# State-space stage of a hybrid encoder step: the samples' state products as four fp32 products on 32 rows each, and the score banks' pair taken as two single banks

## The chip, the cores and the metric

One Trainium2 chip, one of its cores. The metric is the time of one execution on the device in microseconds (us); the kernel before was run three times, and the median counts.

## What is computed

One layer of a streaming encoder runs on 1024 prompt tokens and on 8 samples of 16 tokens. After a modulated norm one projection feeds an attention branch and a state-space branch; the two are merged, projected and added back. The change touches the last line of the state-space scan, as it is done for the samples (one chunk of 16 tokens each, starting from a given state `h0`):

```python
h_new = h * jnp.exp(a_cs[:, -1])[..., None, None] \
    + jnp.einsum('blgn,blgep->bgepn', bk, xdt * to_end[..., None])
```

Per sample and per pair of heads this is a product over 16 tokens: B transposed (128 states by 16 tokens) times the weighted x (16 tokens by 128 values of two heads), added to the decayed state. Everything is float32.

## The kernel before

All tokens of both groups, 1152, lie side by side. The large projections are the bulk of the work: `dense` multiplies one block of 128 output channels at a time, in three groups of 384 tokens (`G3`). Operands are split in two float32r parts (high and low), so that a product is three matmuls for each of the 8 slices of the inner dimension: lines 442, 443 and 445 in the profile. The first two groups of tokens write a bank of the pool `psd` (two banks, tile `d`). The third group, once attention is over (`att_left[0] == 0`), writes one half of the pool `pss` (line 471): one tile `s` of two banks, which attention uses as a pair for its scores. ScalarE, and VectorE behind it, read each group's sums out of the bank: for a convolution's channels lines 1243 and 1244, for the gate z line 1423, for the merge gates line 1355.

Between these matmuls stands the small work. For each of 16 pairs of heads `ssd(p)` has a `main()` that turns x so that tokens lie on partitions (line 1481), builds the prompt's chunk states (L1526), the outputs (L1553, L1560, L1573), and last the samples' new states. These small products use the pool `psg` (four single banks, tile `g`) and are mostly plain fp32.

The samples' 128 tokens (8 of 16) lie on the 128 partitions of `tokb` (B) and `xw` (weighted x). The samples' states are done in four steps `q` of two samples each. Operands are split in high and low parts once more: `hi` and `lo` of B (lines 1496 to 1503, once per group of four pairs, on ScalarE and VectorE), and `xs`, which holds the high part of x on 64 rows and the low part on the other 64 (L1507 on ScalarE, L1508 on VectorE). GpSimd then makes four masked copies of 128x256 (`masked`, L1515) in which all rows but those of one sample are zero, for two samples side by side. A step is two float32r matmuls of all 128 rows by 256 columns (L1598), with B's `hi` and B's `lo`. Steps 0 and 1 fill one bank `g`, steps 2 and 3 another, some microseconds later (`pause(4500)`); after each bank VectorE adds 512 columns to `h0` (L1607), and at the end GpSimd's queue stores `h0` (L1616).

Two things set the order. Python generators write the program: `run` draws from the dense work and lets the small work in by a credit of time, and `pause(...)` holds a piece back. A scheduler then orders each engine's instructions by its own estimate of when they are ready (`schedule_with_timeline_sim=True`). On the chip each engine takes its instructions in that order.

Of the kernel before, what the change touches and what calls it, by code (L numbers as in the profile page):

```python
# [10 lines left out]
ALU = mybir.AluOpType  # L11
# [23 lines left out]
COLS = 53184  # L35
QCOLS = 1024
VCOLS = 6 * 1024
RCOLS = 16 * NT + 4 * 1024 + 1280 + 32
FCOLS = COLS - RCOLS - QCOLS - VCOLS
NQ = 3 * P  # L40

NQL = NQ + 32

C_ID, C_U, C_UB, C_ONE, C_BLK, C_BM, C_SEL, C_S4, C_BM4 = 0, 128, 256, 384, 512, 640, 648, 680, 712
NCONST = 716

PARAMS = [("norm_g", KT), ("b_ada", 24), ("conv_w", NCV * 4), ("conv_b", NCV), ("qk_g", 2), ("dskip", NPAIR),
          ("ssd_g", NPAIR), ("dt_bias", 32), ("a_log", 32)]
# [73 lines left out]
def trunk_kernel(ctx: ExitStack, tc: tile.TileContext, h):  # L122
# [55 lines left out]
    for n, w in PARAMS:  # L178
# [17 lines left out]
    bmask = cst[:, C_BM:C_BM + NB]  # L196
    sel = cst[:, C_SEL:C_SEL + 32]
    sel4 = cst[:, C_S4:C_S4 + 9]
    bmask4 = cst[:, C_BM4:C_BM4 + 4]

    H0 = 0
    W0 = H0 + 16 * NT
# [3 lines left out]
    L_ATT = arena.set_layout(Z0, [("Q", 1, 16 * P), ("T", 5, NT), ("S", 10, 640), ("U", 2, 640), ("K", 4, 512), ("q", 1, 256), ("d", 1, 256),  # L206
                                  ("k", 1, 128), ("p", 1, 128), ("n", 2, 36 + 3 * 16), ("t", 6, 14)])
    L_ATT["Z"] = L_ATT["T"][2:]
    L_SSD = arena.set_layout(Z0, [("X", 1, XW), ("R", 2, 1184), ("t", 8, 36), ("pad", 1, 576), ("T", 9, NT), ("Y", 1, 1184), ("H", 1, 1024),
                                  ("g", 3, G3)])  # L210
    L_HEAD = dict(L_SSD, T=[x for x in L_SSD["T"] if x[0] + x[1] <= Z0 + 7 * NT])
    L_START = arena.set_layout(Z0, [("T", 11, NT), ("ada", 5, 1024), ("e", 2, 256)])
    L_TAIL = arena.set_layout(Z0, [("T", 15, NT)])
# [4 lines left out]
    L_WA = rarena.set_layout(W0, [("w", 2, 1024)])  # L218
    L_QR = rarena.set_layout(W0 + 2 * 1024, [("q", 3, 1024)])
    L_Q = qarena.set_layout(0, [("q", 1, 1024)])  # L220
    L_ST = rarena.set_layout(W0 + 4 * 1024, [("b", 4, P), ("s", 2, P), ("x", 2, 2 * P)])
    L_W3 = varena.set_layout(0, [("w", 2, 3 * 1024)])
    L_W7 = varena.set_layout(0, [("w", 2, 7 * NQL)])
    L_QS = qarena.set_layout(0, [("ada", 1, 1024)])
# [4 lines left out]
    def alloc(lay, tag, cols, cold=None):  # L229
        if lay is L_Q:  # L230
            try:
                return alloc(L_QR, tag, cols)
            except NoSlot:
                pass
        if lay is L_SSD and tag == "H":
            try:
                return Buf(qarena, qarena.alloc(L_QS, "ada", cols), cols)
            except NoSlot:
                pass
        if lay is L_Q or lay is L_QS:  # L240
            return Buf(qarena, qarena.alloc(lay, tag, cols), cols)
        if lay is L_W3 or lay is L_W7 or lay is L_VT or lay is L_VA:
            return Buf(varena, varena.alloc(lay, tag, cols), cols)
        if lay is L_H or lay is L_W or lay is L_WA or lay is L_QR or lay is L_ST:
            return Buf(rarena, rarena.alloc(lay, tag, cols, cold), cols)
        if (lay is L_SSD or lay is L_HEAD or lay is L_TAIL) and tag == "T" or lay is L_HEAD and tag == "Y":
            if v_open[0]:
                try:
                    return alloc(L_VT, "T", cols)
                except NoSlot:  # L250
                    pass
        return Buf(arena, arena.alloc(lay, tag, cols), cols)
# [170 lines left out]
    for x in [h["wall"][i] for i in range(29, 85)] + [h["watt"][i] for i in range(8)] + [h["wssd"][i] for i in range(16)] \  # L423
            + [h["wout"][i] for i in range(8)]:
        job(x)

    def dense(ops, evict, nk=KT, outs=1, last=False, wide=False, order=(0, 1, 2), other=False):

        i = widx[0]
        widx[0] += 1
        hi, lo = yield from w_wait(i)
        if len(jobs[min(i + 1, len(jobs) - 1)]) > 3:
            w_next(i)

        def mm(ps, o, g, k, parts=(0, 1)):
            tok = slice(g * G3, (g + 1) * G3)
            wc = slice((k * outs + o) * P, (k * outs + o + 1) * P)
            kh, kl = ops[k]  # L440
            if 0 in parts:
                nc.tensor.matmul(ps, hi.r[:, wc], kh.r[:, tok], start=k == 0, stop=False)  # L442
                nc.tensor.matmul(ps, hi.r[:, wc], kl.r[:, tok], start=False, stop=False)  # L443
            if 1 in parts:
                nc.tensor.matmul(ps, lo.r[:, wc], kh.r[:, tok], start=False, stop=k == nk - 1)  # L445

        for o in range(outs):
            if wide or (last and o == outs - 1):
                if wide or other:
                    acc = [pg(G3) for _ in range(3)]  # L450
                else:
                    sp = pss.tile([P, 2, 512], F32, tag="s", name=nm("s"))
                    acc = [psd.tile([P, G3], F32, tag="d", name=nm("d")) for _ in range(2)] + [sp[:, 0, :G3]]
                for k in range(nk):
                    while len(ops) <= k:
                        blocked[0] = "operand"
                        yield None
                    for g in range(3):
                        mm(acc[g], o, g, k)
                        if k == nk - 1:  # L460
                            yield from evict(o, g, slice(g * G3, (g + 1) * G3), acc[g]) or ()
                        yield 3 * 162.5
                    if last and o == outs - 1:
                        for x in ops[k]:
                            x.free()
                    if k == 2 and o == 0:
                        w_next(i)
                continue
            for g in order:
                if g == 2 and att_left[0] == 0:  # L470
                    ps = pss.tile([P, 2, 512], F32, tag="s", name=nm("s"))[:, 0, :G3]
                else:
                    ps = psd.tile([P, G3], F32, tag="d", name=nm("d"))
                for k in range(nk):
                    while len(ops) <= k:
                        blocked[0] = "operand"
                        yield None
                    mm(ps, o, g, k)
                    if nk == KT and g == order[-1] and k in (3, 5, 7):
                        w_over(i, k)  # L480
                    yield 3 * 162.5
                yield from evict(o, g, slice(g * G3, (g + 1) * G3), ps) or ()
                if o == 0 and (g == 0 or len(jobs[min(i + 1, len(jobs) - 1)]) > 1):
                    w_next(i)
        w_done(i)
# [876 lines left out]
    grp = {}  # L1362

    def group_dense(g, lay):
        res = grp[g] = {"b": [], "c": [], "sq": None, "st": None}
        yield from conv_gen(16 + g, lay, res["b"])
        yield from conv_gen(20 + g, lay, res["c"])

# [31 lines left out]
    def ssd(p):  # L1400
# [62 lines left out]
        def main():  # L1463
# [24 lines left out]
            me, eb, h0, tm = st["me"]  # L1488
            ssd_all[p + 1] = True

            if res["st"] is None:
                bs = res["st"] = []
                for j in range(2):
                    rw, ro = slice(64 * j, 64 * j + 64), slice(64 - 64 * j, 128 - 64 * j)
                    b_ = tokb.ap[rw, NP:]
                    hi = yield from walloc(L_ST, "b", P)
                    lo = yield from walloc(L_ST, "b", P)
                    nc.scalar.activation(hi.r[rw], b_, AF.Copy)
                    nc.scalar.activation(hi.r[ro], b_, AF.Copy)
                    nc.vector.tensor_tensor(lo.r[rw], b_, hi.ap[rw], ALU.subtract)  # L1500
                    nc.vector.tensor_tensor(lo.r[ro], b_, hi.ap[rw], ALU.subtract)
                    bs.append((hi, lo))
            xs = []
            for j in range(2):
                rw, ro = slice(64 * j, 64 * j + 64), slice(64 - 64 * j, 128 - 64 * j)
                t = yield from walloc(L_ST, "s", P)
                nc.scalar.activation(t.r[rw], xw.ap[rw, NP:], AF.Copy)  # L1507
                nc.vector.tensor_tensor(t.r[ro], xw.ap[rw, NP:], t.ap[rw], ALU.subtract)  # L1508
                xs.append(t)

            def masked(q):

                t = alloc(L_ST, "x", 2 * P)
                i = 2 * (q % 2)
                nc.gpsimd.tensor_tensor(t.r.rearrange("p (b n) -> p b n", n=P), xs[q // 2].ap.unsqueeze(1).to_broadcast([P, 2, P]),  # L1515
                                        bmask4[:, i:i + 2].unsqueeze(2).to_broadcast([P, 2, P]), ALU.mult)
                return t

            xm = [masked(0), masked(1)]

            yield from pause(1500)
            for j in range(2):
# [68 lines left out]
            nc.scalar.activation(z.ap, x.ap, AF.Square)  # L1591
            stored(x)
            yield from pause(2000)
            pss_ = [pg(), pg()]
            for q in range(4):
                j, i = q // 2, q % 2
                for w, b_ in enumerate(res["st"][j]):
                    nc.tensor.matmul(pss_[j][:, 2 * i * P:2 * (i + 1) * P], b_.r, xm[q].r, start=w == 0, stop=w == 1)  # L1598
                xm[q].free()
                if q < 2:  # L1600
                    xm.append(masked(q + 2))
                yield 215
                if q == 1:
                    yield from pause(4500)
                if i:
                    c = slice(4 * j * P, (4 * j + 4) * P)
                    nc.vector.tensor_tensor(h0.ap[:, c], h0.ap[:, c], pss_[j], ALU.add)  # L1607
            for t in xs + [xw]:
                t.free()
            if res["sq"] is None:  # L1610
                res["sq"] = z
            else:
# [4 lines left out]
            stored(h0)  # L1617
            if p % PPG == PPG - 1:
                s = res["sq"]
                for t in (tokb, res["cbm"], res["ct"], *res["st"][0], *res["st"][1]):  # L1620
                    t.free()
                yield from pause(4500)
                r0 = drp.tile([1, NT], F32, name=nm("ya"))
# [301 lines left out]
```

## Time and profile before

| | us |
|---|---|
| three runs | 1956.46, 1957.06, 1957.90 |
| median | 1957.06 |
| span of the profiled execution | 1955.7 |
| TensorE busy in it | 1938.3 |
| state-space stage in it | about 783 to 1530 |

The profile's span runs from the first to the last instruction of one profiled execution. The profile shows no other time of that execution; the median of the runs, which are timed around the whole of it, is 1.4 us longer than this span. PE is TensorE's matmul unit, PEld its weight loads, DVE VectorE, ACT ScalarE, POOL GpSimd. A plain fp32 product is shown as two matmul instructions, a float32r product as one. The duration of a single matmul in the profile is its latency; matmuls overlap, so what one costs is read from the distance between starts.

### The profile page before, as it was taken

Reading aid. Unit: us, or ns where it says so; the run is one execution under the profiler, and the core shown is the slowest. Engines: PE = TensorE matmul, PEld = TensorE weight load, DVE = VectorE, ACT = ScalarE, POOL = GpSimd, SP = SyncE. Lnnn points to the kernel's source line nnn. Section 1 sums busy time; section 2 is a strip of 40 time slices with the busy share of each in tenths; the row PEclk is TensorE's granted clock in tenths of the full one; section 3 lists DMA queues with packets and bytes.
Section 4 is the critical chain, followed back from the end, with each engine's and each line's share of the span. In section 5 each row is a group of like instructions: output and inputs, shape, how many; then the busy total and the mean of one; then the engine's idle time right before and its main releaser. Section 6 shows DMA issues by size and latency. Waiting matters only on the chain.

```text
span 1955.7 us, 35068 instructions
## 1 busy us (share of the span) xinstructions
PE 1938.3 (99%) x14091; PEld 1859.4 (95%) x14091; DVE 1168.5 (60%) x2441; ACT 776.4 (40%) x1589; POOL 323.5 (17%) x624
## 2 busy tenths in 40 slices
PE   7999999999999999999999999999999999999999
PEld 5999999899998999999999999999999999999999
DVE  7455555556555765757566666576674334777732
ACT  8444444445444557344454434345351301111200
POOL 0312213122131201212212221122212100000000
PEclk9999999999999999999999999999999999999999
DMA  9124244232432325433333333332337642331241
GB/s 367 60 81 131 86 132 131 90 122 88 131 112 96 112 88 160 128 112 110 95 132 129 106 103 114 117 118 91 117 118 291 234 140 92 104 104 56 86 143 52
DMA packets 81209, 238.62 MB, mean 122 GB/s; under 512 B 14284, under 2 KB 15320, under 8 KB 81048
## 3 DMA queue, kind: packets, MB, share of 16 engines
q1 hardware_dynamic: 72088, 207.74, 32.7%
q0 software_dynamic: 8960, 28.65, 3.8%
q8 instruction: 111, 1.82, 0.4%
q14 instruction: 50, 0.41, 0.1%
HBM read 192.70 MB, written 43.66 MB: 121 GB/s over the span
## 4 chain that ended last, share of the span: by engine, by line
PE 96%; DVE 1%; ACT 1%; DMA 1%; issue 0%; SPq 0%
PE d L442 13%; PE d L443 13%; PE d L445 13%; PE s L442 5%; PE s L445 5%; PE s L443 5%; PE d L508 5%; PE d L506 5%; PE d L507 5%; PE g L1043 3%; PE g L1066 3%; PE g L1553 2%; PE s L1122 2%; PE g L1526 1%; PE g L1573 1%; PE g L1122 1%
## 5 line engine op out<-in xcount | busy, mean ns | idle before, releaser
L442 PE MATMUL d<-rarena 128*128 128x384 f32 x1520 | 517.4, 340 | 0.3 <-ACT arena L1355 0.3
L445 PE MATMUL d<-rarena 128*128 128x384 f32 x1520 | 511.4, 336 | 0.0
L443 PE MATMUL d<-rarena 128*128 128x384 f32 x1520 | 511.0, 336 | 0.0
L442 PEld LDWEIGHTS d<-rarena 128*128 128x128 f32 x1520 | 285.6, 188 | 4.6 <-issue 2.3
L443 PEld LDWEIGHTS d<-rarena 128*128 128x128 f32 x1520 | 285.6, 188 | 2.8 <-issue 2.4
L445 PEld LDWEIGHTS d<-rarena 128*128 128x128 f32 x1520 | 285.5, 188 | 1.1 <-issue 0.9
L334 ACT ACTIVATE rarena<-arena 128x1024 fp32r<-128x1024 f32 x92 | 97.5, 1060 | 314.1 <-PE s L443 226.2
L442 PE MATMUL s<-rarena 128*128 128x384 f32 x640 | 216.7, 339 | 0.0
L443 PE MATMUL s<-rarena 128*128 128x384 f32 x640 | 214.2, 335 | 0.0
L445 PE MATMUL s<-rarena 128*128 128x384 f32 x640 | 214.1, 334 | 0.0
L508 PE MATMUL d<-va_att,rarena 128*128 128x384 f32 (+1 forms) x559 | 195.0, 349 | 0.0
L506 PE MATMUL d<-va_att,rarena 128*128 128x384 f32 (+1 forms) x559 | 193.9, 347 | 0.0
L507 PE MATMUL d<-va_att,rarena 128*128 128x384 f32 (+1 forms) x559 | 191.0, 342 | 0.0
L335 DVE TENSOR_TENSOR rarena<-arena,rarena 128x1024 fp32r<-128x1024 f32 x92 | 113.2, 1230 | 82.7 <-ACT rarena L334 82.4
L1031 ACT ACTIVATE arena<-arena 128x640 f32<-128x640 f32 (+2 forms) x144 | 101.4, 706 | 138.0 <-DVE arena L1140 99.7
L442 PEld LDWEIGHTS s<-rarena 128*128 128x128 f32 x640 | 120.3, 188 | 1.0 <-issue 1.0
L443 PEld LDWEIGHTS s<-rarena 128*128 128x128 f32 x640 | 120.3, 188 | 0.0
L445 PEld LDWEIGHTS s<-rarena 128*128 128x128 f32 x640 | 120.1, 188 | 0.0
L508 PEld LDWEIGHTS d<-va_att,rarena 128*128 128x128 f32 x559 | 105.5, 189 | 3.9 <-issue 2.7
L1263 DVE SCALAR_TENSOR_TENSOR arena<-arena 128x1176 f32<-128x1176 f32 x66 | 99.9, 1514 | 15.5 <-ACT arena L1260 14.2
L506 PEld LDWEIGHTS d<-va_att,rarena 128*128 128x128 f32 x559 | 105.2, 188 | 3.1 <-issue 1.2
L507 PEld LDWEIGHTS d<-va_att,rarena 128*128 128x128 f32 x559 | 105.2, 188 | 1.0 <-issue 0.4
(345 smaller groups left out, 3212.9 us busy)
## 6 DMA issues: line engine op xcount, KB each, us to landing
arena<-in_wall_dram SPq DMA_DIRECT2D x85, 512.0 KB, 3.9
arena<-in_kc_dram SPq DMA_DIRECT2D x64, 256.0 KB, 4.2
arena<-in_vc_dram SPq DMA_DIRECT2D x64, 256.0 KB, 3.4
arena<-acs_d SPq DMA_DIRECT2D x19, 576.0 KB, 3.8
gate_d<-arena POOLq DMA_DIRECT2D x48, 192.0 KB, 2.5
arena<-y_d SPq DMA_DIRECT2D x15, 576.0 KB, 5.6
arena<-in_wssd_dram SPq DMA_DIRECT2D x16, 512.0 KB, 4.1
arena<-in_wada_dram SPq DMA_DIRECT2D x15, 512.0 KB, 8.9
```

The costliest lines, as they stand in the source:

```text
L334: keep(nc.scalar.activation(hi.r[:, c], b.ap, AF.Copy))
L335: keep(nc.vector.tensor_tensor(lo.r[:, c], b.ap, hi.ap[:, c], ALU.subtract))
L442: nc.tensor.matmul(ps, hi.r[:, wc], kh.r[:, tok], start=k == 0, stop=False)
L443: nc.tensor.matmul(ps, hi.r[:, wc], kl.r[:, tok], start=False, stop=False)
L445: nc.tensor.matmul(ps, lo.r[:, wc], kh.r[:, tok], start=False, stop=k == nk - 1)
L506: nc.tensor.matmul(ps, kh.r[:, tok], wh, start=j == 0, stop=False)
L507: nc.tensor.matmul(ps, kh.r[:, tok], wl, start=False, stop=False)
L508: nc.tensor.matmul(ps, kl.r[:, tok], wh, start=False, stop=j == KT - 1)
L1031: nc.scalar.activation(p, p, AF.Exp, bias=sm_[:, 4 + e:5 + e], scale=-1.0, accum_out=sm_[:, 6 + e:7 + e])
L1043: nc.tensor.transpose(ps[:, s * P:(s + 1) * P], p[:, (j + s) * P:(j + s + 1) * P], ident)
L1122: late(nc.tensor.matmul(banks[k][e][:, o:o + w], x.r[hs, qs], y.r[hs, kk], start=i == 0, stop=i == 2))
L1263: nc.vector.scalar_tensor_tensor(yc, r.ap[:, j:j + n], w4[:, i, j:j + 1], yc, ALU.mult, ALU.add)
```

## The change

The high and low parts of B and x, their layout in the float32r arena, and three of four masked copies go away. GpSimd makes one masked copy `xm` of 128x256 per pair: in each group of 32 rows (two samples) the left 128 columns hold the rows of the first sample and the right 128 those of the second. Four plain fp32 matmuls, one for each group of 32 rows, multiply these 32 rows of B with the same 32 rows of `xm`, each into a bank of its own: three of pool `psg`, and for the fourth one half of the `s` tile. VectorE adds four times 256 columns. The wait of 4500 ns between the halves goes.

`half_pair` allocates the `s` tile once and hands out its two halves in turn, to the fourth product and to the third groups of `dense` in this stage and after it; before, each third group allocated the tile anew and took half 0. The masks and the arenas are sized to fit: 256 columns move from the float32r arena to the plain one. Lines move by 8 to 18: 442, 443, 445 of the kernel before are 452, 453, 455, and the new products are line 1580, their additions 1585.

```diff
+    pair = []
+
+    def half_pair(cols):
+
+        if not pair:
+            sp = pss.tile([P, 2, 512], F32, tag="s", name=nm("s"))
+            pair.extend(sp[:, e, :] for e in range(2))
+        pair.append(pair.pop(0))
+        return pair[-1][:, :cols]
...
                 if g == 2 and att_left[0] == 0:
-                    ps = pss.tile([P, 2, 512], F32, tag="s", name=nm("s"))[:, 0, :G3]
+                    ps = half_pair(G3)
...
-            if res["st"] is None:
-                bs = res["st"] = []
-                for j in range(2):
...
-                    nc.scalar.activation(hi.r[rw], b_, AF.Copy)
-                    nc.scalar.activation(hi.r[ro], b_, AF.Copy)
-                    nc.vector.tensor_tensor(lo.r[rw], b_, hi.ap[rw], ALU.subtract)
-                    nc.vector.tensor_tensor(lo.r[ro], b_, hi.ap[rw], ALU.subtract)
...
-                nc.scalar.activation(t.r[rw], xw.ap[rw, NP:], AF.Copy)
-                nc.vector.tensor_tensor(t.r[ro], xw.ap[rw, NP:], t.ap[rw], ALU.subtract)
-                xs.append(t)
...
-            xm = [masked(0), masked(1)]
+            xm = yield from walloc(lay, "x", 2 * P)
+            nc.gpsimd.tensor_tensor(xm.ap.rearrange("p (b n) -> p b n", n=P), xw.ap[:, NP:].unsqueeze(1).to_broadcast([P, 2, P]),
+                                    parity.unsqueeze(2).to_broadcast([P, 2, P]), ALU.mult)
...
-            pss_ = [pg(), pg()]
-            for q in range(4):
-                j, i = q // 2, q % 2
-                for w, b_ in enumerate(res["st"][j]):
-                    nc.tensor.matmul(pss_[j][:, 2 * i * P:2 * (i + 1) * P], b_.r, xm[q].r, start=w == 0, stop=w == 1)
...
-                if q == 1:
-                    yield from pause(4500)
-                if i:
-                    c = slice(4 * j * P, (4 * j + 4) * P)
-                    nc.vector.tensor_tensor(h0.ap[:, c], h0.ap[:, c], pss_[j], ALU.add)
+            pq = [pg(2 * P) for _ in range(3)] + [half_pair(2 * P)]
+            for r in range(4):
+                rw = slice(32 * r, 32 * r + 32)
+                nc.tensor.matmul(pq[r], tokb.ap[rw, NP:], xm.ap[rw], start=True, stop=True)
+            xm.free()
+            yield 440
+            for r in range(4):
+                c = slice(2 * r * P, 2 * (r + 1) * P)
+                nc.vector.tensor_tensor(h0.ap[:, c], h0.ap[:, c], pq[r], ALU.add)
```

On TensorE, at the second of the 16 pairs, the kernel before has two groups of four products; here is the first (`g` is the bank of steps 0 and 1, `d` the dense work's):

```order
L442 MATMUL d_8704<-rarena 128x384
L443 MATMUL d_8704<-rarena 128x384
L445 MATMUL d_8704<-rarena 128x384
L1598 MATMUL g_8738<-rarena 128x256 x4
L442 MATMUL d_8704<-rarena 128x384
L443 MATMUL d_8704<-rarena 128x384
```

At the same place of the changed kernel stand the four new products, each for 32 rows; `s_7947` is the one `s` tile:

```order
L455 MATMUL d_8678<-rarena 128x384
L1580 MATMUL g_8716<-arena,va_ssd 128x256
L1580 MATMUL g_8717<-arena,va_ssd 128x256
L1580 MATMUL g_8718<-arena,va_ssd 128x256
L452 MATMUL d_8733<-rarena 128x384
L453 MATMUL d_8733<-rarena 128x384
L455 MATMUL d_8733<-rarena 128x384
L1580 MATMUL s_7947<-arena,va_ssd 128x256
L452 MATMUL d_8733<-rarena 128x384
L453 MATMUL d_8733<-rarena 128x384
```

The second group of four is gone, and the fourth new product does not stand with the other three: three dense matmuls were put between. So it is at 11 of the 16 pairs (with 3 to 42 other matmuls between); at the other five, the first, fifth, ninth, fifteenth and sixteenth, the four stand together.

On ScalarE, at the third pair of the kernel before, the reading of the third group's sums (`s`, L1243 and L1244) stands behind a square of 1152 columns, nine pieces of the decay matrix (L1453) and a weight split (L334):

```order
L1457 ACTIVATE arena<-arena 128x1152
L1240 ACTIVATE arena<-d_9046 128x384
L1591 ACTIVATE va_ssd<-arena 128x1152
L1453 ACTIVATE va_ssd<-va_ssd,arena 128x128 x9
L334 ACTIVATE rarena<-arena 128x1024
L1243 ACTIVATE arena<-s_9091 128x256
L1244 ACTIVATE arena<-s_9091 128x8x16
```

In the changed kernel the same reading is L1252 and L1253, the square L1574, the decay matrix L1462:

```order
L1462 ACTIVATE arena<-arena 128x128 x7
L1466 ACTIVATE arena<-arena 128x1152
L1249 ACTIVATE arena<-d_9010 128x384
L1574 ACTIVATE va_ssd<-arena 128x1152
L334 ACTIVATE rarena<-arena 128x1024
L1252 ACTIVATE arena<-s_7947 128x256
L1253 ACTIVATE arena<-s_7947 128x8x16
```

The nine pieces of the decay matrix no longer stand ahead of the reading there; the square and the weight split still do.

More of the change, by code (lines that the diff above doesn't have):

```diff
@@ L37 @@
 VCOLS = 6 * 1024
-RCOLS = 16 * NT + 4 * 1024 + 1280 + 32
+RCOLS = 16 * NT + 5 * 1024 + 32
 FCOLS = COLS - RCOLS - QCOLS - VCOLS
@@ L42 @@
 NQL = NQ + 32
-C_ID, C_U, C_UB, C_ONE, C_BLK, C_BM, C_SEL, C_S4, C_BM4 = 0, 128, 256, 384, 512, 640, 648, 680, 712
-NCONST = 716
+C_ID, C_U, C_UB, C_ONE, C_BLK, C_BM, C_SEL, C_S4, C_PAR = 0, 128, 256, 384, 512, 640, 648, 680, 712
+NCONST = 714
 PARAMS = [("norm_g", KT), ("b_ada", 24), ("conv_w", NCV * 4), ("conv_b", NCV), ("qk_g", 2), ("dskip", NPAIR),
@@ L198, in trunk_kernel @@
     sel4 = cst[:, C_S4:C_S4 + 9]
-    bmask4 = cst[:, C_BM4:C_BM4 + 4]
+    parity = cst[:, C_PAR:C_PAR + 2]
     H0 = 0
@@ L208, in trunk_kernel @@
     L_ATT["Z"] = L_ATT["T"][2:]
-    L_SSD = arena.set_layout(Z0, [("X", 1, XW), ("R", 2, 1184), ("t", 8, 36), ("pad", 1, 576), ("T", 9, NT), ("Y", 1, 1184), ("H", 1, 1024),
-                                  ("g", 3, G3)])
+    L_SSD = arena.set_layout(Z0, [("X", 1, XW), ("R", 2, 1184), ("t", 8, 36), ("x2", 1, 256), ("pad", 1, 320), ("T", 9, NT), ("Y", 1, 1184), ("H", 1, 1024),
+                                  ("g", 3, G3), ("x", 1, 256)])
+    L_SSD["x"] += L_SSD.pop("x2")
     L_HEAD = dict(L_SSD, T=[x for x in L_SSD["T"] if x[0] + x[1] <= Z0 + 7 * NT])
@@ L220, in trunk_kernel @@
     L_Q = qarena.set_layout(0, [("q", 1, 1024)])
-    L_ST = rarena.set_layout(W0 + 4 * 1024, [("b", 4, P), ("s", 2, P), ("x", 2, 2 * P)])
     L_W3 = varena.set_layout(0, [("w", 2, 3 * 1024)])
@@ L243, in alloc @@
             return Buf(varena, varena.alloc(lay, tag, cols), cols)
-        if lay is L_H or lay is L_W or lay is L_WA or lay is L_QR or lay is L_ST:
+        if lay is L_H or lay is L_W or lay is L_WA or lay is L_QR:
             return Buf(rarena, rarena.alloc(lay, tag, cols, cold), cols)
@@ L451, in dense @@
                 else:
-                    sp = pss.tile([P, 2, 512], F32, tag="s", name=nm("s"))
-                    acc = [psd.tile([P, G3], F32, tag="d", name=nm("d")) for _ in range(2)] + [sp[:, 0, :G3]]
+                    acc = [psd.tile([P, G3], F32, tag="d", name=nm("d")) for _ in range(2)] + [half_pair(G3)]
                 for k in range(nk):
@@ L1364, in group_dense @@
     def group_dense(g, lay):
-        res = grp[g] = {"b": [], "c": [], "sq": None, "st": None}
+        res = grp[g] = {"b": [], "c": [], "sq": None}
         yield from conv_gen(16 + g, lay, res["b"])
@@ L1489, in main @@
             ssd_all[p + 1] = True
-            if res["st"] is None:
-                bs = res["st"] = []
-                for j in range(2):
[L1494 to L1497, printed above, removed]
-                    nc.scalar.activation(hi.r[rw], b_, AF.Copy)
-                    nc.scalar.activation(hi.r[ro], b_, AF.Copy)
-                    nc.vector.tensor_tensor(lo.r[rw], b_, hi.ap[rw], ALU.subtract)
-                    nc.vector.tensor_tensor(lo.r[ro], b_, hi.ap[rw], ALU.subtract)
[L1502 to L1508, printed above, removed]
-                xs.append(t)
[L1511 to L1517, printed above, removed]
-            xm = [masked(0), masked(1)]
+            xm = yield from walloc(lay, "x", 2 * P)
+            nc.gpsimd.tensor_tensor(xm.ap.rearrange("p (b n) -> p b n", n=P), xw.ap[:, NP:].unsqueeze(1).to_broadcast([P, 2, P]),
+                                    parity.unsqueeze(2).to_broadcast([P, 2, P]), ALU.mult)
             yield from pause(1500)
@@ L1593, in main @@
             yield from pause(2000)
-            pss_ = [pg(), pg()]
-            for q in range(4):
-                j, i = q // 2, q % 2
-                for w, b_ in enumerate(res["st"][j]):
[L1598 to L1602, printed above, removed]
-                if q == 1:
-                    yield from pause(4500)
-                if i:
-                    c = slice(4 * j * P, (4 * j + 4) * P)
-                    nc.vector.tensor_tensor(h0.ap[:, c], h0.ap[:, c], pss_[j], ALU.add)
-            for t in xs + [xw]:
-                t.free()
+            pq = [pg(2 * P) for _ in range(3)] + [half_pair(2 * P)]
[7 more added lines that the diff above has]
+                nc.vector.tensor_tensor(h0.ap[:, c], h0.ap[:, c], pq[r], ALU.add)
+            xw.free()
             if res["sq"] is None:
@@ L1619, in main @@
                 s = res["sq"]
-                for t in (tokb, res["cbm"], res["ct"], *res["st"][0], *res["st"][1]):
+                for t in (tokb, res["cbm"], res["ct"]):
                     t.free()
@@ L1893 @@
     const[:, C_S4:C_S4 + 32] = (i[:, None] % 32) == np.arange(32)[None, :]
-    const[:, C_BM4:C_BM4 + 4] = (i[:, None] // NS) % 4 == np.arange(4)[None, :]
+    const[:, C_PAR:C_PAR + 2] = (i[:, None] // NS) % 2 == np.arange(2)[None, :]
     ar["const"] = const
```

## Prediction

> **What bounds the kernel now.** I read the page first: the busy times, then the chain of waits that ended last.
>
> ```profile
> span 1955.7 us, 35068 instructions
> PE 1938.3 (99%) x14091; PEld 1859.4 (95%) x14091; DVE 1168.5 (60%) x2441; ACT 776.4 (40%) x1589; POOL 323.5 (17%) x624
> ...
> PE 96%; DVE 1%; ACT 1%; DMA 1%; issue 0%; SPq 0%
> ```
>
> TensorE is busy for 99% of the span and makes 96% of the chain. Since matmuls overlap in this view, "busy" alone doesn't prove that nothing waits. So next come the view of waits, for the matmul unit alone, and the table by stage for the stage that is changed (in it TensorE, its weight loads, VectorE, ScalarE, GpSimd, the granted clock):
>
> ```profile
> PE g L577 <- DMA arena<-in_xT_dram: 8.7, 1, 8.7
> PE g L1481 <- DVE arena L1269: 1.8, 2, 1.4
> ...
> PE d L442 <- ACT arena L1355: 0.3, 1, 0.3
> 783.00:1530.00 747.00, 745.28 (x5307) 735.91 (x5306) 482.96 (x791) 307.58 (x610) 152.67 (x280) 1.00 0.38 127
> ```
>
> In the whole run TensorE waits 8.7 us for the first input and a few times under 2 us. In the changed stage it is busy 745.28 of 747.00 us at full clock. So this kernel's time is the length of TensorE's queue: what the change is worth is how much longer or shorter the row of matmuls gets, and work on other engines counts only where TensorE comes to wait for it.
>
> **What goes from TensorE.** The timeline around one group of four old products (L1598), with 33 dense matmuls ahead of it between 912.52 and 918.24:
>
> ```profile
> 912.52 0.33 PE L442 MATMUL s<-rarena 128*128 128x384 f32 x1
> ...
> 917.89 0.33 PE L443 MATMUL d<-rarena 128*128 128x384 f32 x1
> 918.06 0.33 PE L445 MATMUL d<-rarena 128*128 128x384 f32 x1
> 918.24 0.64 PE L1598 MATMUL g<-rarena 128*128 128x256 f32 x4
> 918.71 0.34 PE L442 MATMUL d<-rarena 128*128 128x384 f32 x1
> 918.89 0.34 PE L443 MATMUL d<-rarena 128*128 128x384 f32 x1
> ```
>
> A dense matmul costs (918.24 - 912.52)/33 = 0.173 us from start to start. The group of four costs 918.71 - 918.24 = 0.47 us, 0.118 each, and nothing around it: the next dense matmul follows at the usual 0.17. There are 128 such matmuls, 32 groups of four: 32 x 0.47 = 15.0 us go. That is all the change can ever gain.
>
> **What comes on TensorE.** 64 plain fp32 products on 32 rows. No product of this kernel uses 32 rows, but three neighbours are there. First, the one matmul in the trace that stands alone among dense ones and uses only 64 rows (in the attention stage):
>
> ```profile
> 664.82 0.33 PE L445 MATMUL d<-rarena 128*128 128x384 f32 x1
> 665.08 0.38 PE L1122 MATMUL g<-rarena 64*128 64x256 f32 x1
> 665.39 0.44 PE L442 MATMUL d<-rarena 128*128 128x384 f32 x1
> 665.67 0.34 PE L443 MATMUL d<-rarena 128*128 128x384 f32 x1
> 665.84 0.34 PE L445 MATMUL d<-rarena 128*128 128x384 f32 x1
> ```
>
> From 664.82 to 665.84 are 1.02 us for three dense matmuls (3 x 0.173 = 0.52) and one float32r product of 256 columns, whose own streaming is 0.118 as above. The rest, 1.02 - 0.52 - 0.118 = 0.38 us, is the price of leaving the full array and coming back: the start is late (0.26 instead of 0.17), the return is late (0.31), and the first dense matmul after it holds the next up (0.28). The old products, on all 128 rows, paid none of that.
>
> Second, plain fp32 products in another partial shape, 32 columns wide, four side by side:
>
> ```profile
> 111.04 0.34 PE L507 MATMUL d<-va_att,rarena 128*128 128x384 f32 x1
> 111.31 1.06 PE L1175 MATMUL s<-arena 128*32 128x512 f32 x8
> 112.19 0.40 PE L1178 MATMUL s<-arena 128*32 128x128 f32 x8
> 112.52 0.44 PE L508 MATMUL d<-va_att,rarena 128*128 128x384 f32 x1
> 112.81 0.33 PE L506 MATMUL d<-va_att,rarena 128*128 128x384 f32 x1
> 112.98 0.34 PE L507 MATMUL d<-va_att,rarena 128*128 128x384 f32 x1
> ```
>
> L1175 is four products of 512 columns, each two instructions (hence x8). All take 112.19 - 111.31 = 0.88 us, so one pass of all four side by side takes 0.44, and at 256 columns 0.22: four new products that run together take two passes, 0.44 us, and so does a single one. The same rows give the toll a second time: 111.04 to 112.98 is 1.94 us, less 0.52 for three dense matmuls, 0.88 for L1175 and a quarter of that, 0.22, for L1178's 128 columns: 0.32.
>
> Third, that groups of rows run side by side at all: in the attention stage two products of 64 rows go together.
>
> ```profile
> 105.54 0.28 PE L1122 MATMUL g<-rarena 64*128 64x256 f32 x2
> 105.66 0.28 PE L1122 MATMUL g<-qa_att,rarena 64*128 64x256 f32 x2
> ```
>
> Two products of 256 columns per 0.12 us is what one of 128 rows costs above. Four groups of rows are not in this trace; four groups of columns are.
>
> Now the count, from the order. At 5 pairs the four products stand together, at 11 the fourth stands apart from the three, in the midst of dense matmuls. That makes 5 + 2 x 11 = 27 departures from the full array, each with one body of 0.44 us and one toll. With the row shape's toll, 0.38: 27 x 0.82 = 22.1 us. Against 15.0 that is **7.1 us more**. With the column shape's toll, 0.32, it is 27 x 0.76 = 20.5, 5.5 us more. I take the first, since its shape is the nearer one.
>
> The Trainium skill, "TensorE: Matmul & The Clock Gate", Part 3 (Packing small matmuls), speaks for such packing: K = 32 on four groups of rows measured 3.07 times the speed of one after another. Not the full four times: by it four products would take an estimated 4 x 0.44/3.07 = 0.57 us, and the sum would grow by about 0.13 us at each of the five whole groups, 0.7 us in all. No run here shows it yet, and the columns' rows above show the full four times.
>
> **What goes and comes elsewhere.** The rows of the old steps on the other engines:
>
> ```profile
> L1515 POOL TENSOR_TENSOR rarena<-rarena,arena 128x256 fp32r<-128x256 f32 x64 | 45.3, 726 | 67.4 <-DVE rarena L1508 40.8 <-PE g L1598 26.5
> L1507 ACT ACTIVATE rarena<-arena 64x128 fp32r<-64x128 f32 x32 | 9.8, 306 | 21.8 <-DVE arena L1485 21.4
> L1508 DVE TENSOR_TENSOR rarena<-arena,rarena 64x128 fp32r<-64x128 f32 x32 | 9.6, 301 | 13.1 <-ACT rarena L1507 12.3
> L1607 DVE TENSOR_TENSOR arena<-arena,g 128x512 f32<-128x512 f32 x16 | 10.9, 682 | 10.2 <-PE g L1598 10.2
> ```
>
> GpSimd loses 48 of 64 masks (48 x 0.73 = 35 us), ScalarE 9.8 and VectorE 9.6 us and the smaller splits of B. VectorE's 32 additions of 512 columns become 64 of 256, each between half of 0.68 and all of it: 0 to 22 us more over 16 pairs. All this I cost at nothing. TensorE's 745 us hide it: VectorE is busy for 483 of 747 us there, ScalarE for 308, GpSimd for 153. The store of `h0` may leave earlier, and nobody waits for it but the buffer.
>
> **The added waits.** The fourth product writes half of the `s` tile. In the order it stands behind the reading of the third group's sums from the *other* half, though the halves are separate banks: the scheduler treats the tile as one. On TensorE everything queued behind it would wait too. The place with the least room is the third and the fourth pair, where 22 dense matmuls and one group of three stand between the end of the third group and the fourth product: 22 x 0.173 + 0.82 = 4.6 us. What the reading took before, at the third pair:
>
> ```profile
> 870.46 0.33 PE L445 MATMUL s<-rarena 128*128 128x384 f32 x1
> ...
> 872.92 2.75 ACT L1453 ACTIVATE va_ssd<-va_ssd,arena 128x128 f32<-128x128 f32 x9 [0.54 <-DMA va_ssd<-acs_d]
> ...
> 876.52 0.36 ACT L1243 ACTIVATE arena<-s 128x256 f32<-128x256 f32 x1
> 876.78 0.26 ACT L1244 ACTIVATE arena<-s 128x128 f32<-128x128 f32 x1
> ```
>
> The sums were read by 877.04, 6.6 us after the last matmul of the group began: 2.0 us too late for the new place. But 2.75 + 0.54 = 3.3 us of it are the nine decay pieces and their wait for a load, which the new order has ahead of that point; without them 3.3 us remain. So I take no wait here, and 2 us for each such place as the far end. In return the next third group waits for VectorE's fourth addition; about 26 dense matmuls (4.5 us) lie between, against 0.68 us of work, and I cost it at nothing too. TensorE's own 1.8 and 0.3 us of waits in the row of waits may go or come back elsewhere: 2 us to either side.
>
> **The sum.** The profiled execution spans 1955.7 us, 1.4 less than the median of 1957.06; nothing around the span changes. 1957.06 + 7.1 = **1964.2 us**.
>
> **Rivals.** A measurement of this kernel can tell about 0.2%, 3.9 us, from no change.
>
> 1. The groups of rows do not run four at a time. If each product's second pass must end before the next product's second starts, four take 5 passes of 0.22, three take 4: 5 x (1.10 + 0.38) + 11 x (0.88 + 0.38 + 0.82) = 30.3, 15.3 us more: 1972.4. Wholly one after another: 5 x (1.76 + 0.38) + 11 x (1.32 + 0.38 + 0.82) = 38.4, 23 us more: 1980.5. Against it: in the columns' rows eight instructions of that very form took the time of two. For it: no row of four row groups. 12%.
> 2. TensorE stands at the fourth product for the other half's reader, or at the third group for the fourth addition. At 2 us at four or more of the 11 split places it is 8 us on top: 1972 or more. For it: ScalarE was 6.6 us late at the third pair. Against: the new order and ScalarE's free time. 8%.
> 3. Not slower: the toll is overlapped where only 32 rows are switched, while the array's rest goes on. Then 27 x 0.44 = 11.9 us replace 15.0: 1954.0, and it decides as soon as a departure costs less than 15.0/27 = 0.56 us. For it: a body of 0.44 is below that. Against: both partial shapes in the trace pay 0.32 to 0.38. To be faster by over 3.9 us it would also need one of the old waits to go. 8%.
> 4. The change doesn't do what it says: if the halves could really be taken in turn, the order would hold the fourth product with the three, and 16 departures at 0.82 would cost 13.1 us, 1.9 less than before: 1955.2. The order shows that it isn't so at 11 pairs; the chip takes instructions in this order. 1%.
>
> **How the numbers follow.** The forecast, 5.5 to 9 us more, has 71%. The range from 1960.5 (the column toll, and 2 us of old waits gone) to 1972.5 (the staircase of rival 1, or four places of rival 2) leaves out rivals 3, 4 and the worst of 1 and 2: about 18%. Slower by over 3.9 us are the forecast and rivals 1 and 2, less a little for the low end: 0.87; within: most of rival 3 and that low end, 0.10; faster: 0.03.
>
> **What would show it.** Right: L1580 in the timeline as four or three products that start within some hundredths of a microsecond, dense matmuls 0.8 us further apart around each of 27 departures, TensorE still 99% busy, and no row for L1580 or line 452 in the view of waits. Wrong: L1580's starts 0.2 or 0.4 us apart (rival 1), a row in which TensorE waits for ScalarE's lines 1253, 1364 or 1432 or for VectorE's 1585 (rival 2), or departures that cost under 0.56 us (rival 3).

## The result

The changed kernel takes 1964.40 us (median of 6 runs, 1964.00 to 1965.41), the kernel before 1957.75 beside it (6 runs). The ratio is 1.0036, with a 95% interval from 1.0025 to 1.0046: slower by 0.36%, 6.65 us.

The page of the changed kernel, the lines that answer to those of before:

```profile
span 1962.2 us, 34923 instructions
PE 1946.4 (99%) x14091; PEld 1851.3 (94%) x14091; DVE 1152.9 (59%) x2425; ACT 760.9 (39%) x1541; POOL 278.2 (14%) x576
...
PE 95%; DMA 2%; DVE 1%; ACT 1%; issue 0%; SPq 0%; POOL 0%; DVEq 0%; ACTq 0%; POOLq 0%
```

The span grew by 6.5 us and TensorE's busy time by 8.1, with the same number of matmuls. ScalarE, VectorE and GpSimd have 16, 16 and 45 us less to do, and the kernel is slower all the same. TensorE's waits:

```profile
PE g L586 <- DMA arena<-in_xT_dram: 8.2, 1, 8.2
PE g L1490 <- DVE arena L1278: 1.4, 2, 0.8
PE s L674 <- ACT rarena L655: 0.9, 1, 0.9
PE s L674 <- DVE rarena L667: 0.9, 1, 0.9
PE g L1052 <- DVE arena L1045: 0.4, 2, 0.3
PE d L702 <- DVE arena L693: 0.4, 1, 0.4
```

No row for the new products (L1580), nor for the dense groups that share their bank (L452): the change added no wait. So the time is in the row of matmuls itself. The timeline at the second pair of the changed kernel:

```profile
826.19 0.34 PE L455 MATMUL d<-rarena 128*128 128x384 f32 x1
826.45 0.71 PE L1580 MATMUL g<-arena,va_ssd 32*128 32x256 f32 x6
827.09 0.44 PE L452 MATMUL d<-rarena 128*128 128x384 f32 x1
827.38 0.34 PE L453 MATMUL d<-rarena 128*128 128x384 f32 x1
827.55 0.34 PE L455 MATMUL d<-rarena 128*128 128x384 f32 x1
827.82 0.69 PE L1580 MATMUL s<-arena,va_ssd 32*128 32x256 f32 x2
828.45 0.44 PE L452 MATMUL d<-rarena 128*128 128x384 f32 x1
828.72 0.34 PE L453 MATMUL d<-rarena 128*128 128x384 f32 x1
828.90 0.34 PE L455 MATMUL d<-rarena 128*128 128x384 f32 x1
```

Three products (x6) and one product (x2) cost the same. From 826.19 to 827.55 are 1.36 us; less 3 x 0.173 for the dense matmuls, 0.84 us. From 827.55 to 828.90 are 1.35, which gives 0.83. The start is late (0.26 instead of 0.17), the first dense matmul afterwards holds the next up (0.28), just as at the lone 64-row product of the attention stage.

A rival is that the price belongs to the change from float32r to plain fp32, and not to the shape. The kernel before has plain fp32 products on the full array among the dense matmuls:

```profile
907.08 0.33 PE L445 MATMUL d<-rarena 128*128 128x384 f32 x1
907.26 0.83 PE L1573 MATMUL g<-va_ssd,arena 128*128 128x128 f32 x6
907.84 0.42 PE L442 MATMUL d<-rarena 128*128 128x384 f32 x1
908.10 0.34 PE L443 MATMUL d<-rarena 128*128 128x384 f32 x1
908.28 0.33 PE L445 MATMUL d<-rarena 128*128 128x384 f32 x1
```

From 907.08 to 908.28 are 1.20 us, less 0.52 for the dense matmuls 0.68 us for six passes. Eight passes at 909.52 take 0.22 us longer in the same reckoning, so a pass is worth 0.11 and six 0.66. Only 0.02 us remain: the full array pays next to nothing for the other type. And the lone 64-row product, float32r like its neighbours, paid the price without any change of type.

Where transposes follow, as at the thirteenth pair, a departure costs a little less:

```profile
1390.68 0.34 PE L455 MATMUL d<-rarena 128*128 128x384 f32 x1
1390.95 0.71 PE L1580 MATMUL g<-arena,va_ssd 32*128 32x256 f32 x6
1391.59 0.66 PE L1490 MATMUL g<-arena 128*128 128x128 f32 x4
```

1391.59 - 1390.68 - 0.173 = 0.74. Over the whole trace: 24 departures of 0.82 to 0.85 and three of 0.73 to 0.74, 22.3 us in sum. Not in this sum is that behind these three the second transpose starts 0.165 us after the first, where 0.109 is usual: 0.2 us in all.

### The profile page after: what moved, and what is told of

It is laid out like the page before. It is cut to its first block, busy times and chain, and to the rows that moved or that the text cites. A ratio compares the mean times of both kernels' runs of the same rounds, so it can differ in the third digit from the quotient of the medians.

```text
span 1962.2 us, 34923 instructions
## 1 busy us (share of the span) xinstructions
PE 1946.4 (99%) x14091; PEld 1851.3 (94%) x14091; DVE 1152.9 (59%) x2425; ACT 760.9 (39%) x1541; POOL 278.2 (14%) x576
## 4 chain that ended last, share of the span: by engine, by line
PE 95%; DMA 2%; DVE 1%; ACT 1%; issue 0%; SPq 0%; POOL 0%; DVEq 0%; ACTq 0%; POOLq 0%
PE d L452 13%; PE d L453 13%; PE d L455 13%; PE s L452 5%; PE s L453 5%; PE s L455 5%; PE d L517 5%; PE d L515 5%; PE d L516 5%; PE g L1052 3%; PE g L1075 3%; PE g L1536 2%; PE s L1131 2%; PE g L1509 1%; PE g L1556 1%; PE g L1131 1%
## 5 line engine op out<-in xcount | busy, mean ns | idle before, releaser
L452 PE MATMUL d<-rarena 128*128 128x384 f32 x1520 | 519.7, 342 | 0.0
L452 PEld LDWEIGHTS d<-rarena 128*128 128x128 f32 x1520 | 285.6, 188 | 8.9 <-issue 6.9
L334 ACT ACTIVATE rarena<-arena 128x1024 fp32r<-128x1024 f32 x92 | 97.5, 1060 | 332.5 <-PE s L453 244.5
L452 PE MATMUL s<-rarena 128*128 128x384 f32 x640 | 216.5, 338 | 0.0
L452 PEld LDWEIGHTS s<-rarena 128*128 128x128 f32 x640 | 120.2, 188 | 2.3 <-issue 2.3
L1272 DVE SCALAR_TENSOR_TENSOR arena<-arena 128x1176 f32<-128x1176 f32 x66 | 95.5, 1447 | 9.9 <-ACT arena L1269 9.5
```

The costliest lines, as they stand in the source:

```text
L334: keep(nc.scalar.activation(hi.r[:, c], b.ap, AF.Copy))
L1272: nc.vector.scalar_tensor_tensor(yc, r.ap[:, j:j + n], w4[:, i, j:j + 1], yc, ALU.mult, ALU.add)
```

## The experiments

Theory: TensorE's queue is the time, and what the change adds to it is a price per departure from the full array, nearly the same for one, three or four products; the pair of banks, tracked as one tile, splits the four at 11 pairs and so makes 27 departures out of 16. Rivals: the products themselves are slow; waits or the altered order elsewhere; the banks' turns. On the chips of the experiments the kernel before ran at 1956.93 (first four experiments) and 1957.03 us (last three). The changed kernel was not run again there; by its ratio it would be at 1964.0 and 1964.1.

**Two true banks.** The pool of the pair is closed after attention and opened again as two tiles of one bank:

```diff
...
         if not pair:
-            sp = pss.tile([P, 2, 512], F32, tag="s", name=nm("s"))
-            pair.extend(sp[:, e, :] for e in range(2))
-        pair.append(pair.pop(0))
-        return pair[-1][:, :cols]
+            pss_pool[0].__exit__(None, None, None)
+            pss_pool[0] = tc.tile_pool(name="psh", bufs=2, space=bass.MemoryType.PSUM)
+            pair.append(pss_pool[0].__enter__())
+        return pair[0].tile([P, 512], F32, tag="h", name=nm("h"))[:, :cols]
```

> The change as it is, but the pair of banks is given back after attention and opened again as two tiles of one bank each, so that the fourth product no longer stands behind the reader of the other bank. In the order the four products now stand together at all 16 pairs: 16 departures from the full array instead of 27. Theory (a departure costs about 0.84 us whether it holds one, three or four products): 22.1 us become 16 x 0.85 = 13.6, so about 8.5 us under the change: 1956 us, 1.5 us or 0.1% under the kernel before. Rival (the loss lies in the products themselves, their fp32 passes on 32 rows, however they are placed): the same 1964 us as the change. Rival (the change loses by waits and by the altered order elsewhere): anything else, with rows in the view of waits.

Measured: 1953.41 us, ratio to the kernel before 0.9981 (0.9972 to 0.9990). Its timeline at the second pair, where line 1582 is the new product and `h` the bank of its own:

```profile
826.32 0.34 PE L457 MATMUL d<-rarena 128*128 128x384 f32 x1
826.58 0.49 PE L1582 MATMUL g<-arena,va_ssd 32*128 32x256 f32 x3
826.60 0.48 PE L1582 MATMUL h<-arena,va_ssd 32*128 32x256 f32 x1
826.90 0.39 PE L1582 MATMUL g<-arena,va_ssd 32*128 32x256 f32 x3
826.92 0.37 PE L1582 MATMUL h<-arena,va_ssd 32*128 32x256 f32 x1
827.23 0.44 PE L454 MATMUL d<-rarena 128*128 128x384 f32 x1
827.51 0.34 PE L455 MATMUL d<-rarena 128*128 128x384 f32 x1
827.69 0.34 PE L457 MATMUL d<-rarena 128*128 128x384 f32 x1
```

All four start within 0.02 us, then their four second passes. 827.69 - 826.32 - 0.52 = 0.85 us for four, where three and one apart cost 0.84 + 0.83. With the same products, and nothing altered but the allocation of the two banks and by it the order, the change turns from 0.36% slower to 0.19% faster: it is the placement that cost the time. Against the change's 1964.0 us it is 10.6 us less, of which the departures are 22.3 - 13.3 = 9.0 (13 of 0.85, three of 0.73) and TensorE's waits 0.5; 1.1 us stay unassigned. The time is also 2.6 us under the expected 1956. The gain on the kernel before is 3.5 us, where the departures alone give 15.2 - 13.3 = 1.9. By the one profiled execution of each, waits that are 1.7 us shorter in sum cover the rest:

```profile
PE g L588 <- DMA arena<-in_xT_dram: 8.6, 2, 8.4
PE s L676 <- ACT rarena L657: 0.9, 1, 0.9
PE s L676 <- DVE rarena L669: 0.9, 1, 0.9
PE g L1492 <- DVE arena L1280: 0.5, 1, 0.5
PE g L1054 <- DVE arena L1047: 0.4, 2, 0.3
PE d L704 <- DVE arena L695: 0.4, 1, 0.4
```

The transposes' wait for a convolution fell from 1.8 to 0.5 us, and the dense work's 0.3 is gone. This wait differs from kernel to kernel here (0.3 to 1.8 us, in one profiled execution of each); why it does was not tried.

**Four banks of the small products' pool.**

```diff
-            pq = [pg(2 * P) for _ in range(3)] + [half_pair(2 * P)]
+            pq = [pg(2 * P) for _ in range(4)]
```

> The change as it is, but the fourth product takes a bank of the small products' pool like the other three, all four banks of that pool at once. In the order the four stand together at all 16 pairs. Theory: like the run with two tiles, 16 departures, about 1956 us, unless the small work that now waits for one of the four banks holds TensorE up; a row for L1581 or for the other small products in the view of waits would show that. Rival (placement doesn't matter): 1964 us.

Measured: 1955.03 us, ratio 0.9987 (0.9978 to 0.9996). The second way of keeping the four together also undoes the loss, though the time is 1.6 us above the two true banks; the departures explain 0.3 of that, and the rest stays open. No row shows TensorE waiting for one of the four banks. All its 16 departures are of the 0.85 kind, since no transposes follow them here: 16 x 0.85 = 13.6 us.

**Half the columns.**

```diff
-                nc.tensor.matmul(pq[r], tokb.ap[rw, NP:], xm.ap[rw], start=True, stop=True)
+                nc.tensor.matmul(pq[r][:, :P], tokb.ap[rw, NP:], xm.ap[rw, :P], start=True, stop=True)
...
-                c = slice(2 * r * P, 2 * (r + 1) * P)
-                nc.vector.tensor_tensor(h0.ap[:, c], h0.ap[:, c], pq[r], ALU.add)
+                c = slice(2 * r * P, (2 * r + 1) * P)
+                nc.vector.tensor_tensor(h0.ap[:, c], h0.ap[:, c], pq[r][:, :P], ALU.add)
```

> Each of the four products multiplies only the left 128 of its 256 columns (the first of its two samples), and only these are added to the state; the other samples' new states are left at their decayed old ones. Still 27 departures. Theory (about 0.43 us of body, two passes of 0.213, and about 0.41 us of toll that doesn't depend on the work): each body halves, 27 x 0.21 = 5.8 us less than the change: 1958.6 us. Rival (all 0.84 us are streaming at a slow rate): 27 x 0.42 = 11.3 us less, 1953. Rival (all of it is a fixed price): 1964.

Measured: 1956.59 us, ratio to the kernel before 0.9996 (0.9987 to 1.0005); against the change's 1964.0 that is 7.4 us less. The timeline at the second pair:

```profile
825.97 0.34 PE L455 MATMUL d<-rarena 128*128 128x384 f32 x1
826.23 0.50 PE L1580 MATMUL g<-arena,va_ssd 32*128 32x128 f32 x6
826.66 0.44 PE L452 MATMUL d<-rarena 128*128 128x384 f32 x1
826.94 0.34 PE L453 MATMUL d<-rarena 128*128 128x384 f32 x1
827.12 0.34 PE L455 MATMUL d<-rarena 128*128 128x384 f32 x1
```

827.12 - 825.97 - 0.52 = 0.63 us, 0.21 less than with 256 columns. Half the columns save 0.21, so if the columns cost in proportion, all of them cost 0.43, and the rest, about 0.41, is paid whatever is computed. A product that stands alone saves the same 0.21 (0.83 to 0.62), which says again that three side by side take the time of one. The time fell by more than the 27 x 0.21 = 5.7 us that this gives; 0.6 us are a shorter wait of the transposes (1.4 to 0.8), and the remainder lies within the two intervals.

**All apart.**

```diff
                 nc.tensor.matmul(pq[r], tokb.ap[rw, NP:], xm.ap[rw], start=True, stop=True)
+                yield from pause(1500)
```

> The change with a pause of 1.5 us in the program after each of the four products, so that dense matmuls stand between all of them: 64 departures with one product each instead of 27. Same products, same work. Theory: 64 x 0.83 = 53 us against 22, 31 us more than the change: 1995 us. Rival (the cost goes with the products): 1964 us.

Measured: 1993.73 us (two runs), ratio 1.0187 (1.0168 to 1.0205), 29.7 us above the change. The timeline of one of the 64:

```profile
828.40 0.34 PE L455 MATMUL d<-rarena 128*128 128x384 f32 x1
828.67 0.69 PE L1580 MATMUL g<-arena,va_ssd 32*128 32x256 f32 x2
829.29 0.44 PE L452 MATMUL d<-rarena 128*128 128x384 f32 x1
829.57 0.34 PE L453 MATMUL d<-rarena 128*128 128x384 f32 x1
829.75 0.34 PE L455 MATMUL d<-rarena 128*128 128x384 f32 x1
```

829.75 - 828.40 - 0.52 = 0.83 us, and 64 of them are 53 us: 31 more than the change's 22.3, less 1.1 us by which the transposes' wait is shorter (1.4 to 0.3). With the same 64 products, 16, 27 and 64 departures gave 1953 or 1955, 1964 and 1994 us.

**Without the products, after and before.** In the changed kernel the products, their additions and their banks are left out; in the kernel before likewise, with its masks kept:

```diff
-            pq = [pg(2 * P) for _ in range(3)] + [half_pair(2 * P)]
-            for r in range(4):
-                rw = slice(32 * r, 32 * r + 32)
-                nc.tensor.matmul(pq[r], tokb.ap[rw, NP:], xm.ap[rw], start=True, stop=True)
             xm.free()
-            yield 440
-            for r in range(4):
-                c = slice(2 * r * P, 2 * (r + 1) * P)
-                nc.vector.tensor_tensor(h0.ap[:, c], h0.ap[:, c], pq[r], ALU.add)
```

> The changed kernel without the samples' four state products and their additions: the samples' states are stored decayed only. The masked copy is still made and the dense groups still take the two halves in turn. Theory: all that TensorE loses by the change lies in the 27 departures, 24 at 0.84 and three ahead of transposes at about 0.66, 22.1 us: 1942 us. Rival (part of the loss is the altered order or the banks' turns): more than 1943 us, and above the kernel before without its products.

> The kernel before without its 128 float32r state products and their additions; splits and masks are still made. Theory: 32 groups of 0.47 us go, 15.0 us: 1942.7 us, the same as the changed kernel without its products. Rival (the old products cost less or more than their rows say, since something else fills their place): not 15 us.

Measured: 1940.98 us (ratio to the kernel before 0.9920, 0.9903 to 0.9936) and 1940.55 us (0.9917, 0.9902 to 0.9932). Without their products the two kernels are the same within the intervals, which are some 3 us to either side. So the splits, the masks, the removed pause and the altered order elsewhere, all that remains different, are worth nothing that four runs of each can tell. By the pages, TensorE's busy time falls by 22.4 and 15.6 us, beside 22.3 and 15.2 from the starts. The times are 1.0 and 2.1 us lower than expected. The transposes' wait is 0.7 and 0.3 us in them instead of 1.4 and 1.8, and the kernel before itself runs 0.7 us faster here than beside the change.

**The banks' turns alone.** The kernel before, with `half_pair` for the dense work's third groups:

```diff
...
-                    ps = pss.tile([P, 2, 512], F32, tag="s", name=nm("s"))[:, 0, :G3]
+                    ps = half_pair(G3)
```

> The kernel before with one part of the change alone: the dense work's third groups take the two halves of the one s tile in turn, the state products are the old ones. Theory: nothing stands behind these banks for long, and the tile is tracked as one either way: the same as the kernel before, 1957.7 us within 1 us. Rival (the turns help by letting a group start earlier, or hurt): more than 2 us to either side.

Measured: 1956.82 us against 1957.03, ratio 0.9998 (0.9989 to 1.0007): no change. TensorE has no wait for these banks in its rows, and taking them in turn by itself neither helps nor hurts by more than about 2 us.

## Why the prediction was right, point by point

**What bounds the kernel.** Right: TensorE's queue. 45 us less work on GpSimd, 16 on ScalarE and 16 on VectorE bought nothing, and the two kernels without their products are equal within their intervals. GpSimd's masks went from 45.3 to 9.7 us, close to the 35 less that were predicted; the other 10 us lie in other rows of GpSimd.

**What goes.** 15.0 us were taken from one group at 0.47; over all 32 the trace of before gives 15.2 (29 of 0.48 and three next to transposes of 0.45 on average). Leaving them out saved 16.5 us, with 2.0 of shorter waits in it.

**What comes.** 27 x 0.82 = 22.1 us were predicted, 22.3 measured. The toll taken from the lone 64-row product held for 32 rows, 0.38 against 0.41, and so did the columns' full fourfold: four products take the time of one. The Trainium skill's 3.07 times ("TensorE: Matmul & The Clock Gate", Part 3, given there for 512 columns) do not appear here: by the estimated 0.57 us of body four products would cost about 0.13 more than one, and they cost 0.85 against 0.83.

**The waits.** Those of the new products were taken at nothing, and there are none. At the third pair, the doubtful place, ScalarE of the changed kernel did this:

```profile
869.07 1.17 ACT L1574 ACTIVATE va_ssd<-arena 128x1152 f32<-128x1152 f32 x1 [3.04 <-DVE arena L1569]
870.14 1.04 ACT L334 ACTIVATE rarena<-arena 128x1024 fp32r<-128x1024 f32 x1
871.09 0.36 ACT L1252 ACTIVATE arena<-s 128x256 f32<-128x256 f32 x1
871.35 0.27 ACT L1253 ACTIVATE arena<-s 128x128 f32<-128x128 f32 x1
```

The last matmul of the third group and the fourth product:

```profile
868.79 0.33 PE L455 MATMUL s<-rarena 128*128 128x384 f32 x1
...
873.72 0.69 PE L1580 MATMUL s<-arena,va_ssd 32*128 32x256 f32 x2
```

The sums were read by 871.62, 2.8 us after that matmul (3.3 were predicted), and the fourth product came 2.1 us later. The wait cost nothing as a wait. It cost 11 departures, since the scheduler put dense work in its place: that was in the prediction's count, read from the order.

**The sum.** +7.1 us predicted, +6.65 measured. The trace has 22.3 - 15.2 = 7.1 in departures, and TensorE's waits went from 13.4 to 12.2 us in sum, 1.2 the other way. That leaves 0.6 of the span's 6.5 us, of which the transposes behind three departures are 0.2; the rest is unassigned. That the forecast of 1964.2 us came so near is in part luck: both terms were sized 0.2 too low and cancel, the shorter waits were not foreseen, and the kernel before, timed again beside the change, had a median 0.7 us higher than the 1957.06 from which the sum starts.

**The rivals.** Rival 1 fell by the starts of the four within 0.02 us, rival 2 by the rows of waits, rival 3 by 0.84 against its limit of 0.56 us. Rival 4 described the kernel with two true banks, and there missed by 1.8 us: 1955.2 forecast, 1953.4 measured, with 1.7 of shorter waits that it didn't know of.

## What to carry to other kernels

Where one engine's queue is the time, count on that engine alone, and price a small matmul from its neighbours' starts, the step out of the full array and back included: here that step costs as much (0.41 us) as all four products together (0.43). So partial shapes should stand together, and what scatters them is as dear as the work; here it was two halves of one tile, which the scheduler held to be one thing, and two true tiles made the change a gain of 0.19%, about half of it from fewer departures and the rest from shorter waits. Read such a split from the order before reading any time.

## What the runs showed of the hardware

Four plain fp32 products on four groups of 32 rows, each into its own bank, start within 0.02 us, and a departure with all four costs 0.85 us where one with a single product costs 0.83. In this shape each of the two passes lasts longer than its columns need: in the kernel with two true banks 826.58 to 826.90 and 826.90 to 827.23, 0.32 and 0.33 us, where a pass of 256 columns is worth 0.21. The lone 64-row product lost about as much in its single pass, 0.31 us for columns worth 0.118, so the loss did not double with the second pass. Plain fp32 products on the full array showed no such toll (0.02 us). What TensorE does in the 0.41 us of a departure, the profile does not show.
